# Expert weights in 16 KB buffers and runs, and the last expert's second weight by halves of its rows

## The chip, the cores and the metric

The kernel runs on one core of a Trainium2 chip. The metric is device time in microseconds (us) of one execution; the span runs from the first to the last instruction that the profile shows. TensorE, VectorE, ScalarE, GpSimd and SyncE are PE, DVE, ACT, POOL and SP in the rows. SP issues almost all transfers.

## The reference

One transformer-like block over 256 tokens of width 1024 (a gated linear recurrence and a spatial gating branch), then a mixture of experts with the top 4 of 32, then a norm. All numbers are fp32. The expert part, which is most of the work:

```python
def expert_block(args):
    xblk, e = args
    z = xblk @ w1[e] + b1[e]                       # 1024 x 2048
    gate = jnp.minimum(z[:, :D_EXPERT], SWIGLU_LIMIT)
    lin = jnp.clip(z[:, D_EXPERT:], -SWIGLU_LIMIT, SWIGLU_LIMIT)
    return (gate * jax.nn.sigmoid(SWIGLU_ALPHA * gate) * (lin + 1.0)) @ w2[e] + b2[e]   # 1024 x 1024
```

Each expert has 8 MiB of w1 and 4 MiB of w2, 384 MiB in all; every expert is computed for its selected tokens (up to 64 in the usual path).

## The kernel before

**The front stage** (up to about 500 us) computes modulation, recurrence, gating, branches, output projection and router. Its weights come in granules of 1 MiB, 1024 rows by 256 columns, that is in runs of 1 KB. A granule is split into a high and a low part by ScalarE and VectorE (L241, L242), which frees its buffer, and is used in 48 products (L321).

**The buffers.** `wtile` hands out 8 KB (per partition) buffers in a fixed rotation, the list `slots`. It begins with three (`ring`); after the third granule of section 6 seven more join it (`ringb`, `LATER` = 3), which lie where the attention's tiles were. At the expert stage four more (`d0` to `d3`) and one for a single use (`big1`) follow when the tiles in them are done, and five of `ringc`, where the front stage's pools were. So 20 MiB can be in before TensorE frees a buffer.

**The expert stage.** For each expert e TensorE opens two accumulators with the bias (L791), multiplies the gathered tokens with eight loads of w1 (`w1_step`, L800, one load is 128 rows by 2048 columns, an 8 KB run on each partition), with the scatter of an earlier expert (L852) and on odd experts the gather for the next two (L769) between them. VectorE and ScalarE make the gated product, meanwhile TensorE multiplies expert e-1 with its four loads of w2 (`w2_steps`, L836, again 8 KB runs), and then turns the gated product of e (L818). The order on TensorE is the order of the code (`manual_schedule`); on SP and the other engines the scheduler sets the order, and SP then issues strictly in it. A load waits on SP until the last reader of its buffer is done, and for the load eight issues before it.

**The last expert's w2** (`last_columns`) comes as four column blocks of 256, each in two half-MiB transfers with 1 KB runs; each block is multiplied (L868), scaled (L871), scattered (L876, L877), squared for the norm on ScalarE (L879) and multiplied by the norm's gain (L880). Then the norm and the output.

Of the kernel before, what the change touches and what calls it, by code (L numbers as in the profile page):

```python
# [8 lines left out]
F32 = mybir.dt.float32  # L9
# [22 lines left out]
def kernel(  # L32
# [174 lines left out]
    def mod_col(j, h, res):  # L207
        a, step = mod_sums(j, h)

        def finish():  # L210
            step(1)
            pt = bank("tp", (P, 4, 2))
            for k in range(4):
                te.matmul(pt[:, k], a[:, k * P:(k + 1) * P], ones[:, 0:2], start=True, stop=True)
            ve.tensor_add(res[:, 4 * h:4 * h + 4], pt[:, :, 0], bmcol[:, 8 * j + 4 * h:8 * j + 4 * h + 4])
        return [lambda: step(0), finish]
# [134 lines left out]

    pack2 = pack_rows("pack2", [(rows(norm2_g), 8), (rows(lb_fwd), 16), (rows(lb_bwd), 16), (rows(gnorm_g), 1), (b_s[0], 8)])
    cols2 = unpack(pack2, "cols2")
    n2col, gncol = cols2[:, 0:8], cols2[:, 40:41]
# [179 lines left out]
    for j in range(5):  # L534
# [22 lines left out]
        if j == 0:  # L557
# [11 lines left out]
            nc.sync.dma_start(wr_sb, w_router[0].rearrange("(k p) e -> p k e", p=P))  # L569
# [20 lines left out]
    def more_slots(n):  # L590
        if n == LATER:
            slots.extend([(ringb, "w")] * RING_B)

    more_slots(0)
# [4 lines left out]
    for j in range(4):  # L599
        pp = two(win(6, j), hT[0], True)  # L600
        more_slots(j + 1)
# [14 lines left out]
    for j in range(4):  # L616
        pp = two(win(5, j), hT[0], False)
        more_slots(j + 5)
# [54 lines left out]
    for j in range(4):  # L673
# [14 lines left out]
        for k in range(2):  # L688
            for tt in range(2):
                te.transpose(pt[:, k, tt * P:(tt + 1) * P], acc[:, tt, (2 * j + k) * P:(2 * j + k + 1) * P], ident)  # L690
# [56 lines left out]
    slots[4:4] = [(consts, f"d{i}") for i in range(4)] + [(consts, "big1")]  # L747
    slots += [(ringc, "w")] * RING_C
# [46 lines left out]
    def w1_step(zz, xT, kt, src):  # L795
        w = wtile([P, 2 * D])
        nc.sync.dma_start(w, src)
        for n in range(2):
            for h in range(2):
                te.matmul(zz[n][h * C:(h + 1) * C], xT[:, kt], w[:, n * D + h * 512:n * D + (h + 1) * 512],  # L800
# [22 lines left out]
    def w2_steps(hT2, selb, w2e):  # L823
# [33 lines left out]
    def last_columns(j, hT2, pT, selb, wcol, w2e):  # L857

        selb = selb.to_broadcast([96, C])
        s = slice(j * 256, (j + 1) * 256)  # L860
        w = wtile([P, KT, 256])
        for h in range(2):
            nc.sync.dma_start(w[:, 4 * h:4 * h + 4], w2e[:, h, :, s])
        py = bank2(("py", "misc")[j % 2], (P, 256))
        te.matmul(py[0:C], selb, b3[:, 2, s], start=True, stop=False, skip_group_check=True)
        for kt in range(KT):
            h = kt % 2
            te.matmul(py[h * C:(h + 1) * C], hT2[:, kt % 4, (kt // 4) * C:(kt // 4) * C + C], w[:, kt],  # L868
                      start=kt == 1, stop=kt >= KT - 2, skip_group_check=True)
        y = wk.tile([P, 256], F32, name="y")  # L870
        ve.tensor_mul(y, py, g2bc[:, s])  # L871

        def rest():
            for tt in range(2):
                pc = bank2((("sc0", "sc1"), ("gate", "lin"))[j % 2][tt], (P, 256))
                te.matmul(pc, pT[:, tt * P:(tt + 1) * P], y, start=True, stop=True)  # L876
                ve.scalar_tensor_tensor(acc[:, tt, s], pc, wcol[tt], acc[:, tt, s], op0=OP.mult, op1=OP.add)  # L877
# [171 lines left out]
```

## Time and profile before

| | |
|---|---|
| median of 3 runs | 1451.46 us (1450.17 to 1451.85) |
| profiled execution | 1452.21 us, span 1450.4 us |
| TensorE busy | 1345.7 us, 93% of the span |
| VectorE, ScalarE, GpSimd busy | 640.0, 307.9, 161.1 us |
| SP's transfers | 483.37 MB, 84.3% of the 16 transfer engines' span |
| mean granted TensorE clock | 0.984 |

A busy share is an average over stages with different limits: the front stage and the expert stage have to be read apart.

### The profile page before, as it was taken

To read this page: it belongs to the slowest core of one execution; us is meant where nothing else is said; L and a number is where in the kernel's file an instruction comes from. 1 tells how busy PE (TensorE), PEld (TensorE's weight loads), DVE (VectorE), ACT (ScalarE), POOL (GpSimd) and SP (SyncE) were. 2 spreads that over 40 slices of the span, in tenths; PEclk is the share of its full clock that TensorE was granted. 3 is DMA by queue.
4 is the path that set the end of the run, shared out by engine and by line. 5 is a ranking of instruction groups with operands and counts; after the bars stand their busy time and mean duration, and the time that the engine had idled before them with its cause. 6 is when DMAs were issued, how large, how long until landed. Compare 5 with 4: busy or idle time off the path is not lost. (4 is left out here: it accounts for less than half of the span.)

```text
span 1450.4 us, 19638 instructions
## 1 busy us (share of the span) xinstructions
PE 1345.7 (93%) x8218; PEld 743.0 (51%) x8218; DVE 640.0 (44%) x1108; ACT 307.9 (21%) x497; POOL 161.1 (11%) x109
## 2 busy tenths in 40 slices
PE   6979798979999999999999999999999999899996
PEld 4979787878999843333333332323323233232323
DVE  5498888887768613222222322222222222222223
ACT  2463354454444310100000000100001000010001
POOL 3054323240064000000000000000000000000001
PEclk8999999999999999999999999999999999999999
DMA  9536252534995899999999999999999999999994
GB/s 333 188 116 204 88 195 67 201 120 162 292 295 220 312 388 414 420 420 421 421 420 420 420 421 420 421 420 421 421 420 421 420 421 422 420 420 421 420 419 173
DMA packets 130751, 487.43 MB, mean 336 GB/s; under 512 B 9161, under 2 KB 71746, under 8 KB 82018
## 3 DMA queue, kind: packets, MB, share of 16 engines
q1 hardware_dynamic: 129810, 483.37, 84.3%
q0 software_dynamic: 848, 2.75, 0.6%
q8 instruction: 66, 1.08, 0.3%
q14 instruction: 27, 0.22, 0.0%
HBM read 485.04 MB, written 1.05 MB: 335 GB/s over the span
## 5 line engine op out<-in xcount | busy, mean ns | idle before, releaser
L800 PE MATMUL gate<-w,xT 128*64 128x512 f32 x1024 | 270.4, 606 | 18.6 <-DMA w<-in_w_dram 17.2
L800 PE MATMUL lin<-w,xT 128*64 128x512 f32 x1024 | 263.5, 592 | 0.0
L836 PE MATMUL py<-w,hT 128*64 128x512 f32 x992 | 228.1, 597 | 20.8 <-DMA w<-in_w_dram 20.8
L321 PE MATMUL acc<-hh,ghi 128*128 128x256 f32 x576 | 166.9, 290 | 12.1 <-ACT iv L394 12.1
L855 DVE SCALAR_TENSOR_TENSOR acc<-sc,wts,acc 128x512 f32<-128x512 f32 x124 | 87.4, 746 | 205.3 <-PE sc L852 205.3
L321 PE MATMUL acc<-hh,glo 128*128 128x256 f32 x576 | 165.5, 288 | 11.3 <-DVE glo L242 11.3
L321 PE MATMUL acc<-hl,ghi 128*128 128x256 f32 x576 | 165.1, 287 | 0.0
L242 DVE TENSOR_TENSOR glo<-w,ghi 128x1024 fp32r<-128x1024 f32 (+1 forms) x99 | 139.1, 1409 | 50.2 <-ACT ghi L241 49.8
L836 PEld LDWEIGHTS py<-w,hT 128*64 128x64 f32 x992 | 66.3, 136 | 162.8 <-issue 98.6
L800 PEld LDWEIGHTS lin<-w,xT 128*64 128x64 f32 x1024 | 74.3, 137 | 145.5 <-issue 145.5
L800 PEld LDWEIGHTS gate<-w,xT 128*64 128x64 f32 x1024 | 61.0, 136 | 163.6 <-issue 96.6
L241 ACT ACTIVATE ghi<-w 128x1024 fp32r<-128x1024 f32 (+1 forms) x102 | 102.4, 1007 | 144.3 <-PE acc L321 106.6
L321 PEld LDWEIGHTS acc<-hh,ghi 128*128 128x128 f32 x576 | 111.4, 194 | 13.3 <-ACT iv L394 12.5
L321 PEld LDWEIGHTS acc<-hh,glo 128*128 128x128 f32 x576 | 111.3, 193 | 13.0 <-DVE glo L242 12.8
L321 PEld LDWEIGHTS acc<-hl,ghi 128*128 128x128 f32 x576 | 111.4, 193 | 0.7 <-issue 0.7
L839 DVE TENSOR_TENSOR y<-py,g2h 128x512 f32<-128x512 f32 x31 | 21.4, 691 | 188.1 <-PE py L836 188.1
L925 POOL DMA_DIRECT2D bc<-in_final_g_dram x1 | 0.6, 557 | 934.3 <-DMA w<-in_w_dram 934.3
L773 ACT ACTIVATE xT<-misc,sh,a 128x128 f32<-128x128 f32 (+1 forms) x68 | 30.7, 451 | 272.4 <-DVE xT L775 272.4
L807 DVE TENSOR_SCALAR g<-gate 128x512 f32<-128x512 f32 x32 | 22.1, 691 | 147.1 <-PE gate L800 147.1
L321 PE MATMUL acc<-ghi,hh 128*128 128x256 f32 x256 | 73.3, 288 | 14.0 <-DVE og L383 6.4
L775 DVE TENSOR_SCALAR xT<-misc,a,sh 128x128 f32<-128x128 f32 (+1 forms) x68 | 27.2, 401 | 131.0 <-PE misc L769 120.5
L808 ACT ACTIVATE s<-g 128x512 f32<-128x512 f32 x32 | 20.2, 630 | 292.5 <-DVE g L807 292.5
(316 smaller groups left out, 1732.4 us busy)
## 6 DMA issues: line engine op xcount, KB each, us to landing
w<-in_w_dram SPq DMA_DIRECT2D x380, 1024.0 KB, 19.8
w<-in_w_in_dram SPq DMA_DIRECT2D x33, 1024.0 KB, 5.6
w<-in_w_mod_dram SPq DMA_DIRECT2D x24, 1024.0 KB, 6.6
w<-in_w_branch_a_dram SPq DMA_DIRECT2D x4, 1024.0 KB, 16.2
w<-in_w_branch_b_dram SPq DMA_DIRECT2D x4, 1024.0 KB, 12.2
w<-in_w_out_dram SPq DMA_DIRECT2D x4, 1024.0 KB
w<-in_w_dram SPq DMA_DIRECT2D x8, 512.0 KB, 8.7
w<-in_w_in_dram SPq DMA_DIRECT2D x12, 256.0 KB, 7.5
```

Of the source, the lines that this page charges most:

```text
L241: sc.activation(hi, src, AF.Copy)
L242: eng.tensor_sub(lo, src, hi)
L321: te.matmul(o, l, r, start=opens and kt == 0 and n == 0, stop=kt == KT - 1 and n == 2, skip_group_check=True)
L773: sc.activation(xT[:, kt], pg[:, k], AF.Identity, bias=sh2[:, kt:kt + 1], scale=a2[:, kt:kt + 1])
L775: ve.tensor_scalar(xT[:, kt], pg[:, k], a2[:, kt:kt + 1], sh2[:, kt:kt + 1], op0=OP.mult, op1=OP.add)
L800: te.matmul(zz[n][h * C:(h + 1) * C], xT[:, kt], w[:, n * D + h * 512:n * D + (h + 1) * 512], start=False, stop=kt == KT - 1, skip_group_c ...
L807: ve.tensor_scalar(g, zz[0], 7.0, None, op0=OP.min)
L808: sc.activation(s, g, AF.Sigmoid, scale=1.702)
L836: te.matmul(py[h * C:(h + 1) * C], hT2[:, kt % 4, (kt // 4) * C:(kt // 4) * C + C], w[:, k, h * 512:(h + 1) * 512], start=False, stop=kt = ...
L839: ve.tensor_mul(y, py, g2h)
L855: ve.scalar_tensor_tensor(acc[:, tt, s], pcs[h], wcol[tt], old[:, tt, s], op0=OP.mult, op1=OP.add)
L925: gp.dma_start(fgbc, bcast(final_g, D))
```

## The change

- At the expert stage the list becomes three double buffers of 16 KB (`ringb`), the three single ones, `d0` to `d3`, `big1`, and three double ones (`ringc`): again 20 MiB. `ringb` no longer serves granules: the front stage keeps three buffers to its end.
- `two_units` loads 2 MiB: as one transfer into a double buffer where the next entry of the list is one, and otherwise as two transfers into two single buffers. `wtile` takes the first entry of the wanted size.
- The rows of w1 are taken in pairs, row 256 j + 2 p + k on partition p, so that a double load has one run of 16 KB on each partition; w2 has it with four rows of 4 KB. A single load still has 8 KB runs. The order of the 1024 inner rows follows in x1's transposes and gathers (read in steps of two elements), in the modulation's columns (`cols3`) and in the router's weights (four transfers).
- The last expert's w2 comes as four blocks of 1 MiB: 512 columns by half of the rows, in 2 KB runs.

The core of the diff:

```diff
-    slots = [(ring, "w")] * RING_A
-
-    def wtile(shape):
-
-        pool, tag = slots.pop(0)
+    slots = [(ring, "w", 1)] * RING_A
+
+    def wtile(shape, units=1):
+
+        i = next(i for i, s in enumerate(slots) if s[2] == units)
+        pool, tag, _ = slots.pop(i)
         if tag != "big1":
-            slots.append((pool, tag))
+            slots.append((pool, tag, units))
         return pool.tile(shape, F32, name="w", tag=tag)
+
+    def two_units(src, n):
+
+        r = 4096 // n
+        if slots[0][2] == 2:
+            w = wtile([P, r, n], 2)
+            nc.sync.dma_start(w, src)
+            return w[:, :r // 2], w[:, r // 2:]
+        ws = [wtile([P, r // 2, n]) for _ in range(2)]
+        for i, w in enumerate(ws):
+            nc.sync.dma_start(w, src[:, i * (r // 2):(i + 1) * (r // 2)])
+        return ws
...
-    def more_slots(n):
-        if n == LATER:
-            slots.extend([(ringb, "w")] * RING_B)
...
-    slots[4:4] = [(consts, f"d{i}") for i in range(4)] + [(consts, "big1")]
-    slots += [(ringc, "w")] * RING_C
+    slots[:] = ([(ringb, "w", 2)] * RING_B + slots + [(consts, f"d{i}", 1) for i in range(4)] + [(consts, "big1", 1)] +
+                [(ringc, "w", 2)] * RING_C)
...
-                    te.matmul(pg[:, k], x1[:, tt, kt * P:(kt + 1) * P], tok[:, tt], start=tt == 0, stop=tt == 1)
+                    te.matmul(pg[:, k], view(x1, tt * D + kt // 2 * 256 + kt % 2, [[2, P]]), tok[:, tt], start=tt == 0, stop=tt == 1)
...
-            w = wtile([P, 2, D])
-            nc.sync.dma_start(w, w2e[:, k2 // 2, k2 % 2 * 2:k2 % 2 * 2 + 2])
+            if k2 % 2 == 0:
+                ws = two_units(w2e[:, k2 // 2], D)
+            w = ws[k2 % 2]
...
-    w1e = lambda e, kt: w1[0, e, kt * P:(kt + 1) * P]
+    w1e = lambda e, j: w1[0, e, j * 256:(j + 1) * 256].rearrange("(p k) n -> p k n", k=2)
...
             for kt in range(KT):
-                w1_step(zz, xTs[e], kt, w1e(e, kt))
+                if kt % 2 == 0:
+                    ws = two_units(w1e(e, kt // 2), 2 * D)
+                w1_step(zz, xTs[e], kt, ws[kt % 2])
...
-        rest = last_columns(0, hT2, pT, sel(e), wcols(e), w2e(e))
+        first, last = (last_columns(c, hT2, pT, sel(e), wcols(e), w2e(e)) for c in range(2))
+        first[0]()
         scatter(*ready[1:])
-        for j in range(1, 4):
-            then = last_columns(j, hT2, pT, sel(e), wcols(e), w2e(e))
-            rest()
-            rest = then
-        rest()
+        first[1]()
+        last[0]()
+        first[2]()
+        last[1]()
+        last[2]()
...
-RING_B = 7
-RING_C = 5
+RING_B = 3
+RING_C = 3
```

In the new `last_columns` the second half of a column block is multiplied and finished in one piece of 512 columns for the first block and in two of 256 for the last.

**The order on SP, end of the front stage.** Before, the last granules (w_out) are issued ahead of the first expert loads; `w` with a number is a load in the order of the code:

```order
L293 DMA w_5132<-in_w_out_dram 128x8x256 [waits DMAHW2_49,DVE_49]
L293 DMA w_5210<-in_w_out_dram 128x8x256 [waits DMAHW3_49,DVE_49]
L293 DMA w_5288<-in_w_out_dram 128x8x256 [waits DMAHW4_49,DVE_49]
L797 DMA w_5503<-in_w1_dram 128x2048 [waits DMAHW5_49,DVE_49]
L797 DMA w_5509<-in_w1_dram 128x2048 [waits DMAHW6_49,DVE_49]
```

Now three double loads of expert 0 stand between the third and the fourth granule of section 5 (w_4137 and w_4208), ahead of 16 further granules:

```order
L306 DMA w_4066<-in_w_in_dram 128x8x256 [waits DMAHW5_49,DMAHW0_49,DVE_49]
L306 DMA w_4137<-in_w_in_dram 128x8x256 [waits DMAHW6_49,DVE_49]
L58 DMA w_5515<-in_w1_dram 128x4096 [waits DVE_49,Pool_49]
L58 DMA w_5525<-in_w1_dram 128x4096 [waits DVE_49,PE_49]
L58 DMA w_5550<-in_w1_dram 128x4096
L306 DMA w_4208<-in_w_in_dram 128x8x256 [waits DMAHW7_49,DVE_49]
L306 DMA w_4279<-in_w_branch_b_dram 128x8x256 [waits DMAHW0_49,DVE_49]
```

Six MiB moved ahead of the fourth granule.

**The order on SP, expert stage.** Before, it is the order of the code; here the four loads of w2 of expert 28 and the first of w1 of expert 30:

```order
L832 DMA w_9336<-in_w2_dram 128x2048 [waits DMAHW5_49,PE_49]
L832 DMA w_9342<-in_w2_dram 128x2048 [waits DMAHW6_49,PE_49]
L832 DMA w_9348<-in_w2_dram 128x2048 [waits DMAHW7_49,PE_49]
L832 DMA w_9354<-in_w2_dram 128x2048 [waits DMAHW0_49,PE_49]
L797 DMA w_9375<-in_w1_dram 128x2048 [waits DMAHW1_49,PE_49]
```

Now the same place (w_9138, w_9139 and the double w_9150 are w2 of expert 28, w_9175 to w_9217 w1 of expert 30, w_9242 to w_9253 w2 of expert 29):

```order
L62 DMA w_9138<-in_w2_dram 128x2048 [waits DMAHW3_49,DMAHW2_49,PE_49]
L58 DMA w_9150<-in_w2_dram 128x4096 [waits PE_49]
L58 DMA w_9175<-in_w1_dram 128x4096 [waits DMAHW4_49,PE_49]
L58 DMA w_9191<-in_w1_dram 128x4096 [waits DMAHW5_49,PE_49]
L58 DMA w_9207<-in_w1_dram 128x4096 [waits DMAHW6_49,PE_49]
L58 DMA w_9217<-in_w1_dram 128x4096 [waits DMAHW7_49,PE_49]
L58 DMA w_9242<-in_w2_dram 128x4096 [waits DMAHW0_49,PE_49]
L62 DMA w_9139<-in_w2_dram 128x2048 [waits DMAHW1_49,PE_49]
L62 DMA w_9252<-in_w2_dram 128x2048 [waits DMAHW2_49,PE_49]
```

w_9139 moved behind six double loads that come after it in the code. The same stands once in each round of the list, 17 times from w_5844 (expert 3) to w_9139; at expert 31 a load, w_9323, stands behind three double loads.

**The order on TensorE, same place.** The products of expert 28's w2 keep the order of the code:

```order
L851 MATMUL py_9135<-w_9138,hT2_9025 64x512 [waits DMAHW2_49]
L851 MATMUL py_9135<-w_9138,hT2_9025 64x512 x3
L851 MATMUL py_9135<-w_9139,hT2_9025 64x512 [waits DMAHW1_49]
L851 MATMUL py_9135<-w_9139,hT2_9025 64x512 x3
L851 MATMUL py_9135<-w_9150,hT2_9025 64x512 [waits DMAHW3_49]
```

Nothing moved here: TensorE waits for w_9139 ahead of w_9150.

## Rows read from the trace of the kernel before

**Rows 1.** The page's head and slices of 36 us.
```profile
span 1450.4 us, 19638 instructions
...
GB/s 333 188 116 204 88 195 67 201 120 162 292 295 220 312 388 414 420 420 421 421 420 420 420 421 420 421 420 421 421 420 421 420 421 422 420 420 421 420 419 173
```

**Rows 2.** Stretches: length, busy PE, PEld, DVE, ACT, POOL, clock, transfer share, GB/s.
```profile
384.00:400.00 16.00, 16.00 (x139) 16.00 (x138) 12.81 (x16) 7.06 (x11) 0.00 (x0) 1.00 1.09 348
600.00:800.00 200.00, 200.00 (x968) 71.60 (x966) 56.76 (x100) 15.30 (x28) 0.00 (x0) 1.00 1.01 421
...
1000.00:1100.00 100.00, 91.48 (x419) 29.77 (x417) 24.16 (x41) 6.11 (x11) 0.00 (x0) 1.00 1.01 421
```

**Rows 3.** TensorE in order of time, experts 5 and 6, and L940.
```profile
634.03 0.41 PE L791 MATMUL gate<-b,sel 96*64 96x512 bf16 x2
...
655.45 7.03 PE L836 MATMUL py<-w,hT 128*64 128x512 f32 x32
662.41 0.75 PE L818 MATMUL misc<-ident,l 128*128 128x128 f32 x4
663.09 0.41 PE L791 MATMUL gate<-b,sel 96*64 96x512 bf16 x2
...
687.89 0.41 PE L791 MATMUL gate<-b,sel 96*64 96x512 bf16 x2
...
1403.24 1.13 PE L940 MATMUL misc<-g2h,ident 128*128 128x512 f32 x2
```

**Rows 4.** TensorE in order of time, later.
```profile
851.38 0.75 PE L818 MATMUL misc<-ident,l 128*128 128x128 f32 x4
...
1420.88 1.94 PE L836 MATMUL py<-w,hT 128*64 128x512 f32 x8 [0.62 <-DMA w<-in_w_dram]
1422.74 0.75 PE L818 MATMUL misc<-ident,l 128*128 128x128 f32 x4
```

**Rows 5.** The page's issues: count, size of one, median us to landing.
```profile
w<-in_w_dram SPq DMA_DIRECT2D x380, 1024.0 KB, 19.8
```

**Rows 6.** The page's packets, counted up to each size.
```profile
DMA packets 130751, 487.43 MB, mean 336 GB/s; under 512 B 9161, under 2 KB 71746, under 8 KB 82018
```

**Rows 7.** SP's issues in order of time.
```profile
371.75 12.00 SPq L293 DMA_DIRECT2D w<-in_w_branch_b_dram  x4
...
436.07 60.45 SPq L797 DMA_DIRECT2D w<-in_w_dram  x16
500.77 2.08 SPq L832 DMA_DIRECT2D w<-in_w_dram  x4
```

**Rows 8.** TensorE in order of time, expert 1's last w1 product.
```profile
546.31 1.03 PE L800 MATMUL lin<-w,xT 128*64 128x512 f32 x4
```

**Rows 9.** The w1 loads of L797 by source.
```profile
DMA to landing us min/median/max: 4.8/19.8/21.4
```

**Rows 10.** ScalarE's splits in order of time.
```profile
371.72 1.06 ACT L241 ACTIVATE ghi<-w 128x1024 fp32r<-128x1024 f32 x1 [1.26 <-PE acc L321]
...
385.85 1.06 ACT L241 ACTIVATE ghi<-w 128x1024 fp32r<-128x1024 f32 x1 [1.78 <-PE acc L321]
...
393.37 1.06 ACT L241 ACTIVATE ghi<-w 128x1024 fp32r<-128x1024 f32 x1 [2.21 <-issue]
```

**Rows 11.** Stretches around a gap of TensorE in the front stage.
```profile
100.00:104.00 4.00, 3.33 (x17) 3.37 (x18) 4.00 (x5) 0.62 (x2) 2.74 (x2) 0.54 0.00 0
104.00:108.00 4.00, 4.00 (x36) 4.00 (x35) 4.00 (x7) 2.63 (x6) 0.00 (x0) 1.00 0.00 0
```

**Rows 12.** TensorE in order of time, first and last products at the lower clock.
```profile
100.67 0.55 PE L321 MATMUL acc<-ghi,hh 128*128 128x256 f32 x1 [6.37 <-DVE og L383]
...
103.57 0.32 PE L321 MATMUL acc<-ghi,hl 128*128 128x256 f32 x1
```

**Rows 13.** First product of the last blocks, and VectorE's start of the norm.
```profile
1424.18 1.95 PE L868 MATMUL py<-w,hT 128*64 128x256 f32 x16 [0.25 <-ACT hT L820]
...
1441.68 0.16 DVE L1000 TENSOR_REDUCE fss<-ss 128x2 f32<-128x8 f32 x1 [0.64 <-ACTq L960]
```

More of the change, by code (lines that the diff above doesn't have):

```diff
@@ L350 @@
             dense(g, four_outs(pps, natural), natural, ((2 * q, 2),), ve if q else gp)
+    pack3 = late.tile([12, 256], F32, name="pack3")
+    for i, src in enumerate((norm2_g[0], b_mod[0, 3 * D:4 * D], b_mod[0, 4 * D:5 * D])):
+        nc.sync.dma_start(pack3[4 * i:4 * i + 4], src.rearrange("(r f) -> r f", f=256))
+    cols3 = consts.tile([P, 3, KT], F32, name="cols3")
+    pt = bank("tp", (P, 2, 12))
+    for k in range(2):
+        te.transpose(pt[:, k], view(pack3, k, [[2, P]]), ident[:12, :12])
+    ve.tensor_copy(cols3.rearrange("p i (j k) -> p i j k", k=2), pt.rearrange("p k (i j) -> p i j k", i=3))
+    n2col = cols3[:, 0]
     pack2 = pack_rows("pack2", [(rows(norm2_g), 8), (rows(lb_fwd), 16), (rows(lb_bwd), 16), (rows(gnorm_g), 1), (b_s[0], 8)])
     cols2 = unpack(pack2, "cols2")
-    n2col, gncol = cols2[:, 0:8], cols2[:, 40:41]
+    gncol = cols2[:, 40:41]
     lb, omlb = [], []
@@ L855, in scatter, with last_columns @@
                 ve.scalar_tensor_tensor(acc[:, tt, s], pcs[h], wcol[tt], old[:, tt, s], op0=OP.mult, op1=OP.add)
-    def last_columns(j, hT2, pT, selb, wcol, w2e):
+    def last_columns(c, hT2, pT, selb, wcol, w2e):
         selb = selb.to_broadcast([96, C])
[L860 to L871, printed above, removed]
-        def rest():
[L874 to L877, printed above, removed]
-                junk = wk.tile([P, 256], F32, name="junk", tag="g", bufs=1)
-                sc.activation(junk, acc[:, tt, s], AF.Square, accum_out=ss8[:, tt, j:j + 1])
-                (gp if j < 3 else ve).tensor_mul(accg[:, tt, s], acc[:, tt, s], fgbc[:, s])
-        return rest
@@ new lines, in last_columns, with products @@
+        py = bank2(("py", "misc")[c])
+        y = wk.tile([P, 512], F32, name="y")
+        blocks = [slice(0, 512)] if c == 0 else [slice(0, 256), slice(256, 512)]
+        def products(u):
+            if u == 0:
+                te.matmul(py[0:C], selb, b3[:, 2, c * 512:(c + 1) * 512], start=True, stop=False, skip_group_check=True)
+            w = wtile([P, 4, 512])
+            nc.sync.dma_start(w, w2e[:, u, :, c * 512:(c + 1) * 512])
+            for b in blocks if u else [slice(0, 512)]:
+                for k in range(4):
+                    h = k % 2
+                    te.matmul(py[h * C:(h + 1) * C, b], hT2[:, k, u * C:u * C + C], w[:, k, b],
+                              start=u == 0 and k == 1, stop=u == 1 and k >= 2, skip_group_check=True)
+                if u:
+                    ve.tensor_mul(y[:, b], py[:, b], g2bc[:, c * 512 + b.start:c * 512 + b.stop])
@@ new lines, in rest @@
+        def rest():
+            for i, b in enumerate(blocks):
+                n = b.stop - b.start
+                s = slice(c * 512 + b.start, c * 512 + b.stop)
+                for tt in range(2):
+                    pc = bank2((("sc0", "sc1"), ("gate", "lin"))[(c + i) % 2][tt], (P, n))
+                    te.matmul(pc, pT[:, tt * P:(tt + 1) * P], y[:, b], start=True, stop=True)
+                    ve.scalar_tensor_tensor(acc[:, tt, s], pc, wcol[tt], acc[:, tt, s], op0=OP.mult, op1=OP.add)
+                    junk = wk.tile([P, n], F32, name="junk", tag="g", bufs=1)
+                    sc.activation(junk, acc[:, tt, s], AF.Square, accum_out=ss8[:, tt, c + i:c + i + 1])
+                    (ve if i else gp).tensor_mul(accg[:, tt, s], acc[:, tt, s], fgbc[:, s])
@@ L883 @@
+        return [lambda: products(0), lambda: products(1), rest]
     tok, xTs = {}, {}
@@ L922 @@
                 slots[:] = [x for x in slots if x[1] not in ("d0", "d1")]
+                assert slots[0][2] == 2 or sum(x[2] == 1 for x in slots) >= 2
                 bc = consts.tile([P, 2, D], F32, name="bc", tag="d0")
@@ L992 @@
         for tt in range(2):
-            for j in range(4):
-                s = slice(j * 256, (j + 1) * 256)
-                junk = wk.tile([P, 256], F32, name="junk", tag="g", bufs=1)
+            for j, s in enumerate((slice(0, 512), slice(512, 768), slice(768, 1024))):
+                junk = wk.tile([P, s.stop - s.start], F32, name="junk", tag="g", bufs=1)
                 sc.activation(junk, acc[:, tt, s], AF.Square, accum_out=ss8[:, tt, j:j + 1])
@@ L1014 @@
 FIRST = 6
-LATER = 3
 MOD_POOL = (0,)
```

24 lines of the change are left out of this document (11 added, 13 removed).

## The prediction

> **What bounds the kernel now.** I first read the page's slices. From about 500 us to 1430 us the transfers run at 419 to 422 GB/s [rows 1]: the expert stage streams its weights at one rate to the end. The windows then show that this is not TensorE's bound at first: from 600 to 800 us TensorE is busy all the time at the same 421 GB/s, from 1000 to 1100 us only 91.48 of 100 us [rows 2]. So the first experts eat a stock of loads that are already there, and after it is used up each product waits for its load. The timeline of TensorE shows both. Without waits two experts take 687.89 - 634.03 = 53.86 us, 2.24 us for each of 24 loads of 1 MiB; the one with gathers takes 29.06 us, the one without 24.80 us [rows 3]. Later the group of L836 at 1420.88 stands behind a wait of 0.62 us for its load, and from the turn (L818) of expert 12 at 851.38 to that of expert 31 at 1422.74 there are 571.36 us for 19 experts, 2.506 us a load [rows 4]. After 1420.88 no load is late: the rest (29.5 us of the span) is a chain of TensorE, VectorE and ScalarE.
>
> Two further facts matter. Loads land in the order of issue: the median from issue to landing is 19.8 us, eight times 2.49 us [rows 5], and each load waits for the eighth before it. And an 8 KB run is one packet: 130751 - 82018 = 48733 packets are of 8 KB or more [rows 6], and 380 loads of 128 rows are 48640.
>
> **The rate: what a 16 KB run saves.** The trace has no run of 16 KB. It has 1 KB runs at 348 GB/s (384 to 400 us) and 8 KB runs at 421 GB/s, both with the transfer engines full [rows 2]. One engine of 16 thus takes 1024/21.75 = 47.1 ns and 8192/26.3 = 311.3 ns for a packet: 0.03686 ns a byte and 9.35 ns a packet. With 16 KB runs a MiB has 4 packets fewer on each engine, 0.0374 us saved of 2.506. Bounds: nothing (a run is cut in two packets), and 0.075 us (the packet's cost vanishes). I take 0.0374, what the two rows give. The Trainium skill (DMA: Bandwidth & Descriptors, section Why small descriptors are slow) puts the fixed overhead at some 3 cycles a packet. At that page's 850 MHz these are 3.5 ns, an estimate by which a MiB would save 0.014 us and the sum below would end at 1467.8 in place of 1463.1; the rows do not agree with it (9.35 ns), and I go by them.
>
> **The order: what the buffers do to it.** 114 double loads carry 228 of the 380 MiB; 152 stay single. The seven single buffers come round on their own, so the eighth single load in a round reuses the buffer of the first. The order on SP shows what becomes of that: the load is put behind the next six double loads, 12 MiB after its place, while TensorE still asks for it in its old place. So TensorE waits at this load until it lands, finds the next 12 MiB there, works through them without a wait (2.24 us each against some 2.48 of the stream), and waits again at the next such load. A round is 20 MiB: the stream needs 20 x 2.506 - 12 x 0.037 = 49.7 us, TensorE 44.9, so it idles some 4.8 us a round, at one place instead of at most loads. While rounds follow each other this costs nothing. It costs at the end: at the last late load that TensorE waits for (w_9139, the second MiB of expert 28's second weight, the 366th MiB in the order of issue, 14 from the end) it is some 13 MiB behind the stream, and no waits are left to lose.
>
> When does w_9139 land? I anchor the stream where it is held by TensorE. Six MiB go ahead of the front stage's last granules, at 371.75 us, when the attention's memory is free; in the kernel before the first expert load goes out at 436.07 and 20 are out at 502.85 [rows 7]. So the stock is full earlier, but it is the same 20 MiB, and then the stream follows the releases. By about 546 us 33 MiB are in (the 20, the last of them issued at about 501 us as before, and 13 whose buffers expert 0 and the first half of expert 1 free); the next double load needs the buffer read by expert 1's last two w1 products, released at 546.31 + 1.03 = 547.3 [rows 8]. The kernel before has, counted back from 1420.9 at 2.506 us, 32 MiB in at that time: a lead of about 1 MiB is all that the early start leaves. From issue to a first landing the least is 4.8 us [rows 9], 2.3 more than the transfer.
>
> The six MiB also delay granules in the front. The fourth granule of section 5 follows them: its buffer is free after a split that starts at 371.72 (about 374.4 with VectorE's part), but its transfer begins when 6 x 2.46 us after 373.0 are over, so it lands at 391.6. Its split, at 385.85 in the kernel before, ends at 394.1; its products begin when the copy at 393.37 can [rows 10]. So I count 0.7 us of delay. Bounds: 0, and 5 us if the following granules are late too; those are issued up to three granules ahead and need 3.0 us of transfer each (1 MiB at 348 GB/s), so I take 0.7.
>
> The sum: 547.3 + 0.7 + 2.3 + 333 MiB x 2.506 (834.5) - 204 MiB x 0.0374 (7.6) = 1377.2 us for w_9139. Behind it TensorE has three MiB of L836 (6.97/4 = 1.74 each, from 655.45 to 662.41: 5.2), the turn (0.68), expert 30 without gathers (24.80) and expert 31, the same with two products of L940 (2 x 1.05) [rows 3]: 57.6 us, to 1434.8. No load is late in it: the 14 MiB behind it and the four last blocks are there by about 1425. The same point of the kernel before is 1422.74 + 0.68 = 1423.4: **11.4 us later**.
>
> The clock: after 6.37 us idle, the products from 100.67 us on come at a granted 0.54 (1.2 GHz), and 1.00 (2.4 GHz) is back 2.9 us later [rows 11, 12]: about 1.4 us lost. A wait of 4 to 5 us may do it; in all rounds but the last the next wait absorbs it. Between 0 and 1.4 I take 0.7.
>
> **The tail.** From 1424.18 to 1441.68 the kernel before has TensorE and VectorE in turn, and its eight half-MiB loads are not waited for [rows 13]. The four new blocks have the same products in groups of 512 columns, two openings with the bias fewer, and the last two 256-column pieces end in the same chain of VectorE and ScalarE. I take -0.5 us; bounds -2 and +1.5.
>
> **Costed at nothing:** x1 read in steps of two elements (gathers and router: hidden in the 4.8 us of a round, and none is in the last 57.6 us), pack3 and the four router loads (front; TensorE is busy there and waits for none of them), the gates' place in it.
>
> Sum: 11.4 + 0.7 - 0.5 = +11.6 on a span of 1450.4, 1462.0. The profiled execution took 1452.21, 1.81 more than its span and 0.75 over the median of the runs: as a median, **1463.1 us**.
>
> **The rivals.**
> - *The late loads hold nobody* (faster). If they landed ahead of the double loads, the stream alone would decide: its last MiB at 550.3 + 347 x 2.506 - 210 x 0.0374 = 1412.0, 8.9 us ahead of 1420.9, and with the tail 1442. For it: TensorE is busy without a break up to 800 us [rows 2]. Against it: the landing times [rows 5] and the wait written on w_9139's product. It decides if w_9139 is there 11.6 us earlier, by 1365.6.
> - *The run of 16 KB saves little*, cut in two or limited elsewhere: 7.6 us back, 1470.7. For it: two run lengths always lie on one line, so nothing in the trace proves the line up to 16 KB. Against it: nothing in the trace splits a run of 8 KB. (By the Trainium skill's 3 cycles, named above, it would be the 1467.8.)
> - *The packet's cost vanishes*: 1455.4.
> - *The front is held* by the six MiB for 5 us in place of 0.7: 1467.4.
>
> **How the numbers follow.** The forecast (1458 to 1468) has 0.52, little saving 0.20, late loads harmless 0.12, packet cost gone 0.08, front held 0.06, something else 0.02. The range reaches from the vanishing packet cost less 2 us of tail, 1453, to no saving and the tail's upper bound, 1472, and leaves out the harmless order. Slower by over 0.2% (2.9 us, about what can be told from no change) is above 1454.4: 0.82; within it 0.06; faster 0.12.
>
> **What would show it.** Right: TensorE's waits for weights are some 16 to 18 of 3 to 7 us, at single loads, from about 630 us on; windows near 426 GB/s where double loads pass; no wait on a load after about 1377 us, and the transfers idle from about 1425. Wrong: many waits of 0.5 us up to 1410 us (loads not late), an unchanged 421 GB/s, or a first expert product several us later than in the kernel before.

## The result, and the profile after

The changed kernel takes 1473.45 us (median of 4 runs, 1467.77 to 1474.9), the kernel before beside it 1450.82 (1450.06 to 1451.85): a ratio of 1.0148, with a 95% interval of 1.012 to 1.0176. The direction is that of the forecast, the size is twice it (+22.6 us in place of +11.6). The ratios, here and below, are not the quotients of the medians (here that would be 1.0156); the two differ by up to 0.15%. The profiled execution took 1474.9 us, the slowest of the four; its span is 1473.1 against the 1450.4 of before.

The page of the changed kernel: head, slices of 37 us, packets, and the expert loads with their size and the median time to landing.

```profile
span 1473.1 us, 19304 instructions
...
GB/s 333 183 112 203 88 197 89 170 133 154 333 213 233 328 403 381 426 423 422 426 426 423 422 426 426 420 424 427 423 423 423 426 408 422 426 426 423 423 332 33
DMA packets 111781, 487.42 MB, mean 331 GB/s; under 512 B 6821, under 2 KB 65322, under 8 KB 77642
...
w<-in_w_dram SPq DMA_DIRECT2D x114, 2048.0 KB, 15.9
w<-in_w_dram SPq DMA_DIRECT2D x156, 1024.0 KB, 16.1
```

A 16 KB run is one packet: 111781 - 77642 = 34139 are of 8 KB or more, and 114 double and 152 single loads of 128 runs are 34048 (before: 48733 [rows 6]). Slices of 426 and 422 alternate where [rows 1] had 420 and 421. So the streaming did become faster, and the kernel is slower all the same.

Stretches of the changed kernel, with the same columns as [rows 2]:

```profile
380.00:400.00 20.00, 18.27 (x154) 17.88 (x154) 13.85 (x29) 8.54 (x11) 2.20 (x4) 1.00 0.95 351
400.00:420.00 20.00, 18.63 (x157) 18.43 (x156) 17.02 (x13) 7.47 (x8) 15.45 (x12) 1.00 0.78 257
600.00:800.00 200.00, 191.61 (x905) 69.88 (x903) 52.55 (x98) 15.91 (x30) 0.00 (x0) 0.97 1.01 424
1000.00:1100.00 100.00, 94.44 (x455) 34.94 (x453) 26.01 (x49) 7.94 (x15) 0.00 (x0) 0.98 1.01 424
1384.00:1388.00 4.00, 2.15 (x8) 0.73 (x10) 0.07 (x1) 0.00 (x0) 0.00 (x0) 0.89 1.01 420
1388.00:1392.00 4.00, 4.00 (x16) 1.27 (x14) 0.00 (x0) 0.00 (x0) 0.00 (x0) 0.68 1.02 424
```

The first two in the kernel before:

```profile
380.00:400.00 20.00, 20.00 (x173) 20.00 (x172) 16.16 (x27) 9.60 (x13) 0.00 (x0) 1.00 1.09 348
400.00:420.00 20.00, 20.00 (x168) 19.83 (x168) 14.51 (x12) 8.21 (x9) 13.25 (x10) 1.00 1.05 335
```

Three things are new. TensorE, which in the kernel before is busy for all 40 us from 380 to 420, has 3.1 us of holes there. From 600 to 800 us, where it had no wait at all [rows 2], it is idle for 8.4 us. And the granted clock, 1.00 before, is 0.97 there; from 1388 to 1392 us, behind a wait, its mean is 0.68, so a part of this stretch is at 1.2 GHz and the rest at 2.4.

TensorE in order of time, at the places that set the end:

```profile
396.33 1.16 PE L640 MATMUL o_ps<-wsT,v 128*128 128x128 f32 x8 [0.78 <-DVE t L643]
...
398.67 0.39 PE L334 MATMUL acc<-hh,glo 128*128 128x256 f32 x1 [0.95 <-DVE glo L255]
...
413.18 0.39 PE L334 MATMUL acc<-hl,ghi 128*128 128x256 f32 x1 [1.37 <-DVE hl L255]
...
513.20 1.08 PE L814 MATMUL gate<-w,xT 128*64 128x512 f32 x4
...
520.21 2.10 PE L785 MATMUL misc<-p,acc 128*128 128x64 f32 x16
...
533.63 1.11 PE L832 MATMUL misc<-ident,l 128*128 128x128 f32 x4 [2.12 <-DVE l L825]
...
535.52 1.87 PE L814 MATMUL gate<-w,xT 128*64 128x512 f32 x4
...
555.11 7.03 PE L851 MATMUL py<-w,hT 128*64 128x512 f32 x32
...
590.95 1.08 PE L814 MATMUL gate<-w,xT 128*64 128x512 f32 x4 [1.06 <-DMA w<-in_w_dram]
...
640.83 8.14 PE L851 MATMUL py<-w,hT 128*64 128x512 f32 x24 [3.69 <-DMA w<-in_w_dram]
...
1336.12 1.97 PE L814 MATMUL gate<-w,xT 128*64 128x512 f32 x4 [4.55 <-DMA w<-in_w_dram]
...
1385.85 7.07 PE L851 MATMUL py<-w,hT 128*64 128x512 f32 x24 [1.97 <-DMA w<-in_w_dram]
1392.85 0.75 PE L832 MATMUL misc<-ident,l 128*128 128x128 f32 x4
...
1444.86 0.75 PE L832 MATMUL misc<-ident,l 128*128 128x128 f32 x4
```

The kernel before, at the same gather between the first w1 products and at the turn of expert 0 with the product behind it:

```profile
514.82 2.00 PE L769 MATMUL misc<-p,acc 128*128 128x64 f32 x16
...
528.04 0.75 PE L818 MATMUL misc<-ident,l 128*128 128x128 f32 x4 [2.12 <-DVE l L811]
...
529.17 1.03 PE L800 MATMUL gate<-w,xT 128*64 128x512 f32 x4
```

The late loads are there as forecast: TensorE waits for a load at 590.95 us, at 640.83 and from there every 49.67 us on average up to w_9139 at 1385.85 (15 rounds in 745.02 us; one of them, near 690 us, shows no wait), and no load is waited for behind it. The waits are 0.4 to 6.1 us long, where 3 to 7 were forecast. But everything is later than forecast: the first w1 product comes at 513.20 (507.81 before), w_9139 lands 8.7 us behind the 1377.2 of the sum, and the 24 products behind it take 7.07 us in place of 5.2.

### One table for all runs

The executions of this kernel differ by some us in the early front stage, whatever is changed in the expert stage: the same program text there had its first w1 product at 507.81 in the kernel before and at 513.83 in the run tail_only below. The difference lies early: counted from the last products of the attention (L506, at 359.11 and 364.98 us) it comes after 148.70 us in the one and 148.85 in the other. So the runs are compared by stretches between fixed instructions: point A is the start of the first w1 product, B that of expert 0's first w2 product, C that of the last turn (expert 31). Each row is one profiled execution, read from the order in time of TensorE as above (changed kernel: 513.20, 555.11, 1444.86).

| kernel | A | A to B | B to C | C to end | median us |
|---|---|---|---|---|---|
| before | 507.81 | 39.91 | 875.02 | 27.66 | 1450.82 |
| changed | 513.20 | 41.91 | 889.75 | 28.24 | 1473.45 |
| even_singles | 515.49 | 42.00 | 871.73 | 27.98 | 1457.86 |
| runs_8k | 512.51 | 41.94 | 896.28 | 27.57 | 1481.97 |
| loads_behind | 507.18 | 41.91 | 888.05 | 27.96 | 1467.25 |
| tail_only | 513.83 | 39.92 | 874.68 | 28.27 | 1452.66 |
| even_behind | 507.26 | 40.30 | 870.77 | 27.47 | 1452.78 |
| interleaved | 507.75 | 40.31 | 875.06 | 27.58 | 1455.42 |
| all_double | 505.34 | 40.31 | 872.41 | 27.94 | 1451.28 |
| filled_waits | 511.98 | 41.54 | 891.15 | 28.03 | 1473.02 |
| all_double_early | 518.49 | 41.56 | 874.21 | 27.64 | 1455.20 |
| filled_short | 513.32 | 40.37 | 888.38 | 28.03 | 1473.16 |
| before_less | 503.96 | 41.55 | 877.67 | 27.82 | 1453.85 |
| even_halves | 515.21 | 41.92 | 870.47 | 27.80 | 1450.10 |

The change costs 5.4 us ahead of A, 2.0 from A to B, 14.7 from B to C and 0.6 behind C: 22.7 us. The forecast had 0.7, 0, 11.4 (0.7 of it for the clock) and -0.5.

### The profile page after: what moved, and what is told of

Read it like the earlier page. It is cut to its first block, busy times and chain, and to the rows that moved or that the text cites. A ratio compares the mean times of both kernels' runs of the same rounds, so it can differ in the third digit from the quotient of the medians.

```text
span 1473.1 us, 19304 instructions
## 1 busy us (share of the span) xinstructions
PE 1355.8 (92%) x8190; PEld 756.0 (51%) x8190; DVE 642.2 (44%) x1106; ACT 307.8 (21%) x493; POOL 160.3 (11%) x107
## 2 busy tenths in 40 slices
DMA packets 111781, 487.42 MB, mean 331 GB/s; under 512 B 6821, under 2 KB 65322, under 8 KB 77642
## 5 line engine op out<-in xcount | busy, mean ns | idle before, releaser
L814 PE MATMUL gate<-w,xT 128*64 128x512 f32 x1024 | 275.3, 617 | 39.6 <-DMA w<-in_w_dram 39.6
L814 PE MATMUL lin<-w,xT 128*64 128x512 f32 x1024 | 269.8, 606 | 0.0
L851 PE MATMUL py<-w,hT 128*64 128x512 f32 x992 | 223.9, 603 | 10.5 <-DMA w<-in_w_dram 10.5
L334 PE MATMUL acc<-hh,ghi 128*128 128x256 f32 x576 | 167.9, 292 | 10.3 <-ACT iv L416 10.3
L255 DVE TENSOR_TENSOR glo<-w,ghi 128x1024 fp32r<-128x1024 f32 (+1 forms) x99 | 137.0, 1388 | 56.7 <-ACT ghi L254 56.3
L814 PEld LDWEIGHTS gate<-w,xT 128*64 128x64 f32 x1024 | 65.1, 139 | 176.2 <-issue 116.4
L851 PEld LDWEIGHTS py<-w,hT 128*64 128x64 f32 x992 | 70.1, 139 | 143.5 <-issue 122.4
L334 PEld LDWEIGHTS acc<-hh,ghi 128*128 128x128 f32 x576 | 111.8, 194 | 11.6 <-ACT iv L416 10.7
L785 PEld LDWEIGHTS misc<-p,acc 128*128 128x128 f32 x544 | 67.5, 199 | 28.2 <-issue 27.5
```

The lines of the kernel that those rows point to most:

```text
L255: eng.tensor_sub(lo, src, hi)
L334: te.matmul(o, l, r, start=opens and kt == 0 and n == 0, stop=kt == KT - 1 and n == 2, skip_group_check=True)
L785: te.matmul(pg[:, k], view(x1, tt * D + kt // 2 * 256 + kt % 2, [[2, P]]), tok[:, tt], start=tt == 0, stop=tt == 1)
L814: te.matmul(zz[n][h * C:(h + 1) * C], xT[:, kt], w[:, 0, n * D + h * 512:n * D + (h + 1) * 512], start=False, stop=kt == KT - 1, skip_grou ...
```

## The experiments

### even_singles: no late loads

```diff
-        if tag != "big1":
+        if tag not in ("big1", "d3"):
             slots.append((pool, tag, units))
```

> The changed kernel, with the buffer d3 used for one load only, like big1. The six single buffers left then come round in pairs of the same round, no single load reuses a buffer that was filled seven loads ago, and the loads on SP stand in the order of the code. Stock in the later rounds: 18 MiB in place of 19. Theory A (the late single loads at the end of the stage are what costs): TensorE waits a little at most loads, and the stream's end decides. In the changed kernel w_9139, the 366th MiB, lands at 1385.85; 14 MiB more at 2.47 us end at 1420.4, the last products and the turn at about 1423 instead of 1445.5, so the median falls by some 22 us to about 1451 (1447 to 1455). Rival B (late loads hold nobody, the time went into the front and the clock): within 3 us of 1473. Rival C (half of it): the single that is gone makes the stream wait for TensorE: 1458 to 1468, with windows of the transfers below 415 GB/s.

Measured: 1457.86 us (12 runs; 1.0035 of the kernel before, 1.0015 to 1.0055). TensorE in order of time, the end:

```profile
1425.64 3.65 PE L851 MATMUL py<-w,hT 128*64 128x512 f32 x16 [1.31 <-DMA w<-in_w_dram]
1429.22 0.75 PE L832 MATMUL misc<-ident,l 128*128 128x128 f32 x4
```

TensorE again waits a little at many loads up to the last, and B to C falls by 18.0 us, from 889.75 to 871.73; the median falls by 15.6. So the late loads are what costs, as theory A has it: rival B is out, and the sign of rival C, transfers below 415 GB/s, is not there (425 from 600 to 800 us). The median misses the theory's 1447 to 1455 all the same: of the 22 us expected, 4 are missing from B to C, 2.65 of them for the MiB of stock given up (before_less, below). Point A is no earlier than in the changed kernel (this profile has it 2.3 later): the front is a cost of its own.

### runs_8k: the price of a packet

```diff
-            nc.sync.dma_start(w, src)
+            for i in range(2):
+                nc.sync.dma_start(w[:, i * (r // 2):(i + 1) * (r // 2)], src[:, i * (r // 2):(i + 1) * (r // 2)])
```

> The changed kernel, same buffers and same places on SP, but each double buffer is filled by two transfers of 1 MiB whose runs are 8 KB. Theory (a 16 KB run saves one packet's cost, 0.0374 us a MiB): 204 MiB of double loads ahead of w_9139 cost 7.6 us more, windows fall from 426 to 421 GB/s where double loads pass, median about 1481 (1478 to 1484). Rival (16 KB runs save little): 1473 plus or minus 2, windows unchanged. Rival (the packet's cost vanishes, 0.075 us a MiB): 1488. The number of loads that may be under way is eight in both, here eight MiB in place of up to sixteen; if that matters the slower side shows it too, as holes between loads in the windows.

Measured: 1481.97 us (6 runs; 1.0213, 1.0178 to 1.0248), within the theory's 1478 to 1484. Stretches:

```profile
600.00:800.00 200.00, 187.73 (x900) 69.17 (x900) 52.55 (x98) 15.91 (x30) 0.00 (x0) 0.98 1.01 420
1000.00:1100.00 100.00, 93.19 (x445) 34.56 (x443) 25.09 (x47) 7.94 (x15) 0.00 (x0) 0.97 1.01 419
```

420 and 419 GB/s where the changed kernel has 424. The waits at both ends of the fifteen rounds:

```profile
640.98 5.37 PE L852 MATMUL py<-w,hT 128*64 128x512 f32 x24 [3.67 <-DMA w<-in_w_dram]
...
1393.42 5.37 PE L852 MATMUL py<-w,hT 128*64 128x512 f32 x24 [1.10 <-DMA w<-in_w_dram]
```

The fifteen rounds between the same waits take 752.44 us (640.98 to 1393.42) in place of 745.02, with 180 MiB of double loads in them: 7.42/180 = 0.041 us a MiB, where the line through the runs of 1 KB and 8 KB had given 0.0374. The term of the sum was right in size. What it is the price of is not separated: the edit doubles the packets and the transfers alike. In favour of the packets: the line through the runs of 1 KB and 8 KB, both in transfers of 1 MiB, gives nine tenths of it. The 0.014 us that the Trainium skill's 3 cycles a packet give (DMA: Bandwidth & Descriptors, section Why small descriptors are slow; an estimate at that page's 850 MHz) would have been 2.5 us over these rounds; the measured 7.42 decides against it.

### loads_behind: the front

```diff
         ve.tensor_mul(m, pp, t)
+        if j < 3:
+            w = ringb.tile([P, 2, 2 * D], F32, name="w", tag="w")
+            ve.tensor_copy(w[:, 0, 0:1], m[:, 0, 0:1])
+            nc.sync.dma_start(w, w1[0, 0, j * 256:(j + 1) * 256].rearrange("(p k) n -> p k n", k=2))
```

The three are handed out first, and the list of buffers then begins with the single ones and ends with these three.

> The changed kernel, with the first three double loads tied behind the first three products with branch_a in the front stage (one element of each buffer is written from their result first), so that six MiB no longer stand ahead of the fourth granule of section 5. Theory (the six MiB hold the front): TensorE has no gaps between 390 and 415 us, the first product with w1 comes at 508 to 509 us in place of 513.2, the late loads stay, and the median falls by the same 4 to 5 us to about 1469. Rival (three buffers for granules alone hold the front, not the loads): first product at 511 us or later, median within 2 us of 1473. Rival (the loads come too late for expert 0): the first product is early but TensorE waits at loads ahead of 560 us, and the gain is lost.

Measured: 1467.25 us (5 runs; 1.0096, 1.0063 to 1.0128). Stretches:

```profile
380.00:400.00 20.00, 20.00 (x173) 20.00 (x172) 15.62 (x23) 9.73 (x14) 0.00 (x0) 1.00 0.51 162
400.00:420.00 20.00, 20.00 (x169) 20.00 (x168) 15.31 (x14) 7.07 (x8) 15.00 (x13) 1.00 0.77 238
```

The 40 us have no hole, with the same three buffers for granules, and A is at 507.18. Counted from the last products of the attention (L506, L528 and L532, at 359.11, 359.51 and 357.77 us), A comes after 148.7 us in the kernel before, 153.7 in the changed one and 149.4 here. The other kernels agree: 153.6 to 154.3 us in the four with the six MiB in their early place, 148.6 to 149.8 in the seven without. So it is the six MiB, with 4.3 of the 5.0 us, and not the three buffers by themselves. The median falls by 6.2 us. In the changed kernel SP's issues come in this order:

```profile
370.36 2.29 SPq L58 DMA_DIRECT2D w<-in_w_dram  x3
374.58 0.38 SPq L306 DMA_DIRECT2D w<-in_w_in_dram  x1
380.22 24.23 SPq L306 DMA_DIRECT2D w<-in_w_branch_b_dram  x4
```

and ScalarE's splits follow:

```profile
383.57 1.06 ACT L254 ACTIVATE ghi<-w 128x1024 fp32r<-128x1024 f32 x1 [1.30 <-PE acc L334]
...
394.02 0.60 ACT L636 ACTIVATE t<-acc 128x512 f32<-128x512 f32 x1 [2.73 <-DVE t L643]
...
395.29 1.99 ACT L254 ACTIVATE ghi<-w 128x1024 fp32r<-128x1024 f32 x2
```

The granule behind the six MiB goes out at 374.58. Its split begins at 395.29, where the kernel before has it at 385.85 [rows 10] and the sum had it end at 394.1; VectorE's part ends at 398.61, and the product that waits for it starts at 398.67. The next four splits come 4.4 to 6.7 us later than in the kernel before, and the products stall three times up to 413.18 (3.1 us; the rest of the 5.0 does not show as holes). In the kernel before, with ten buffers, the granules behind it had been on their way (335 GB/s from 400 to 420 us, 257 here). This link between the six MiB and the stalls is read from the rows and not tested by itself; the order of work has a part in it, since ScalarE takes the split only behind an operation for which it waits until 394.02.

### tail_only: the last blocks

The new last_columns, with its order of calls, in the kernel before (the two last parts of the diff, nothing else).

> The kernel before, with nothing of the change but the last expert's second weight in four 1 MB blocks of 512 columns by half of the rows. From the end of the last turn to the end of the span the kernel before takes 27.0 us. The prediction's step: -0.5 us (bounds -2 and +1.5), median about 1450.3. The changed kernel's own trace says 27.6 us: +0.6, 1451.4. Rival (the larger pieces put more of the chain behind the last product): +1.5 us or more, 1452.5. All three are within what a measurement can tell; the profile's stretch from the turn to the end decides.

Measured: 1452.66 us (0.9999, 0.998 to 1.0017), and C to end 28.27 us against 27.66, as the changed kernel's 28.24. The gain of 0.5 us is not there. Whether the new blocks cost something cannot be told: the table has 27.5 to 28.3 us behind C for the kernels with them, and 27.7 and 27.8 for the two without.

### even_behind: both repairs

The diffs of even_singles and loads_behind together.

> Both repairs together: the first three double loads tied behind products with branch_a, and d3 used for one load only, so that the singles come in pairs and no load is late. Measured apart: 1473.45 with neither, 1467.25 with the first, 1457.9 with the second. Theory (two separate causes, which add): 1457.9 - 6.2 = 1451.7, or up to 2 us less, because the run with the second alone had its first w1 product at 515.5 us, 2.3 later than the changed kernel: 1449 to 1452, no different from the kernel before. Rival (the early loads and the late ones are one cause, a fuller stock): 1456 or more. If the 16 KB runs bring what the windows say (0.041 us a MiB on two thirds of the loads, some 9 us), the turn of expert 31 would come ahead of the 1423.4 of before by what is not lost to two MiB less stock (4 to 5 us) and to the last load being 2 MiB long (1.7 us).

Measured: 1452.78 us (1.0019, 1.0003 to 1.0035). The causes add: A as in loads_behind, B to C near that of even_singles (870.77 and 871.73). Against the kernel before, B to C is 4.25 us shorter. By the page it has 127 double loads; some 230 MiB of them fall in this stretch (an estimate: two rounds less than all), worth some 9.5 us at 0.041. So over 5 us were given back; the last two runs ask where.

### interleaved: late by less

```diff
+            if e == 2:
+                s1, s2 = [x for x in slots if x[2] == 1], [x for x in slots if x[2] == 2]
+                slots[:] = (s2[0:1] + s1[0:2] + s2[1:2] + s1[2:4] + s2[2:3] + s1[4:6] + s2[3:4] + s1[6:7] + s2[4:6])
```

on top of loads_behind.

> The three double loads tied behind branch_a as in the run before, all 19 MiB of buffers kept, and from expert 2 on the list of buffers interleaved (double, two singles, double, two singles, ...). On SP one single load a round then stands behind three double loads (6 MiB) in place of six (12 MiB), some others behind one. Theory (what a late load costs is what TensorE is behind the stream at the last of them): about half of the 15.6 to 22 us that taking all late loads away brings, on 1467.25: 1454 to 1460. Rival (any late load costs alike): 1467 plus or minus 2. Rival (late by three doubles is hidden by the stock): 1448 to 1452.

Measured: 1455.42 us (1.0032, 1.0015 to 1.005), within the theory's 1454 to 1460. B to C is 875.06: 13 us less than with loads six doubles late (888.05), 4.3 more than with none (870.77). The last of the late loads:

```profile
1367.73 3.44 PE L860 MATMUL py<-w,hT 128*64 128x512 f32 x8 [3.87 <-DMA w<-in_w_dram]
```

even_behind has a MiB of stock less. With the 2.65 us that before_less gives for it, lateness by three doubles costs some 7 us and by six some 20 (an estimate), and 1.5 of the 7 are the clock, since the 8 products take 3.44 us in place of 1.94. So the dose matters: half the lateness costs about a third, by this one run.

### all_double and all_double_early: nine double buffers

Nothing but double buffers, the front's single ones in a pool that is given up (early: that pool and the others in another order).

```diff
-    ring = ctx.enter_context(tc.tile_pool(name="ring", bufs=RING_A))
+    ring = p1.enter_context(tc.tile_pool(name="ring", bufs=RING_A))
+    dd = p1.enter_context(tc.tile_pool(name="dd", bufs=1))
...
+    slots[:] = [(ringc, "w", 2)] * RING_C + [(ringc, "x", 2)] + [(ringb, "w", 2)] * RING_B
```

> The loads tied behind branch_a, and all weight buffers of the expert stage double (nine, 18 MiB: the singles of the front stage lie in a pool that is given up for them); the last two loads of expert 30's second weight are issued in halves of 1 MiB, the four last blocks go into halves of two double buffers. No load is late. Theory: every MiB gains the 0.041 us that the runs of 8 KB against 16 KB showed: 347 MiB x 0.041 = 14.2 us ahead of the kernel before, 5 us lost to two MiB less of stock, the turn of expert 31 at about 1413 to 1415, median 1441 to 1444. Rival (the stream no longer bounds: TensorE waits 2 to 3 us at each double load): 1448 or more. Rival (the nine buffers come free too late at the start, 500 us in place of 470): first w1 product on time, but waits ahead of 600 us, 1450 or more.

> The kernel with nine double buffers, with its pools in another order, so that the six doubles of ringc lie first on the memory of the front stage's tiles and granules that are done earliest. In the run before, the transfers stood idle from 480 to 500 us (0 and 191 GB/s) with only four double loads issued, and then ran without a hole from 502 us to the end, so the stock was never full. Theory (the missing stock of some 5 to 6 MiB is what kept 0.041 us a MiB from showing): the transfers run at 390 GB/s or more from 480 to 500 us, holes appear between 530 and 560 us (the stock is full), the turn of expert 31 comes 6 to 12 us earlier than 1418.7, median 1439 to 1446. Rival (the rate gain ends at TensorE, which needs 27 us for the last expert whatever is there): the waits get shorter, the turn at 1416 or later, median 1449 or more. Rival (the new place makes the first expert's small tiles wait): first w1 product later than 508 us.

Measured: 1451.28 us (1.0007, 0.9991 to 1.0022) and 1455.20 (1.003, 1.0009 to 1.0052). The first, in stretches:

```profile
480.00:490.00 10.00, 10.00 (x88) 10.00 (x86) 5.24 (x8) 4.07 (x12) 0.00 (x0) 1.00 0.00 0
490.00:500.00 10.00, 9.81 (x70) 7.51 (x69) 6.15 (x30) 3.26 (x7) 0.00 (x0) 1.00 0.53 191
...
530.00:560.00 30.00, 30.00 (x155) 12.02 (x151) 7.50 (x16) 3.06 (x6) 0.00 (x0) 1.00 1.01 426
600.00:800.00 200.00, 196.93 (x947) 70.71 (x945) 55.48 (x99) 14.67 (x27) 0.00 (x0) 1.00 1.01 426
```

The rate is 426 GB/s (0.041 us a MiB off the 421 of before would make 428), but the transfers stand idle just ahead of the expert stage, because the buffers come free too late (SP waits there 15.6 us for VectorE's part of a split and 9.1 for products of the front), and run without a hole afterwards: the stock is never full, and TensorE is idle for 3.1 us between 600 and 800 us, where it was not in the kernel before. B to C is 2.6 us better than before, where 9 were expected (14 less 5 for two MiB of stock). The other pool order did not cure it; the idle stretch moved, and SP waits in it 26.6 us for the router's products:

```profile
490.00:500.00 10.00, 10.00 (x86) 10.00 (x86) 7.05 (x10) 5.42 (x13) 0.00 (x0) 1.00 0.23 95
500.00:510.00 10.00, 10.00 (x81) 9.27 (x81) 4.72 (x16) 3.60 (x11) 0.00 (x0) 1.00 0.01 2
```

Both expectations missed; the rival of all_double, buffers that come free too late, is what the stretches show. That a full stock would bring the gain stays open.

### filled_waits and filled_short: the clock

```diff
+    def fill(n):
+        t = bank2("misc")
+        for _ in range(n):
+            te.matmul(t, ident, g2h, start=True, stop=True)
...
+            if e == 0:
+                fill(4)
...
+            if late and k2 == 1:
+                fill(4)
```

(fill(2) in filled_short; late is expert 28.)

> The changed kernel with four more fp32 products of 128x512 (2.1 us, their result is not used) on TensorE in two of its waits: behind the last w1 product of expert 0 (2.12 us idle there, after which the changed kernel's products take 1.87 us in place of 1.03) and ahead of w_9139's product (1.97 us idle, after which 24 products take 7.07 us in place of 5.2). Theory (TensorE's clock falls to 1.2 GHz in these waits, and this costs 1.9 us at each place that no later wait absorbs): both groups run at 2.4 GHz, the end is 2 to 4 us earlier, about 1470. Rival (it is not the wait that lowers the clock): the same slow products, and 1473 to 1475.

> As the run with filled waits, with two fp32 products in place of four. There, four took 3.70 us in place of the 2.1 meant, so that they reached 1.5 us past the wait; the products behind them did run at the full clock (24 in 5.37 us in place of 7.07). Two take 1.85 us and end ahead of the load. Theory: full clock behind both waits and nothing pushed back: 1.7 to 2.0 us at each place, 1473.4 less 3 to 4 is 1469.5 to 1470.5. Rival (the 0.1 to 0.3 us left idle, or the front, decide): 1473 plus or minus 1.

Measured: 1473.02 and 1473.16 us. TensorE of filled_short in order of time:

```profile
1381.55 1.98 PE L841 MATMUL misc<-g2h,ident 128*128 128x512 f32 x4
1384.76 5.37 PE L859 MATMUL py<-w,hT 128*64 128x512 f32 x24 [1.23 <-DMA w<-in_w_dram]
1390.07 0.74 PE L832 MATMUL misc<-ident,l 128*128 128x128 f32 x4
```

The 24 products take 5.37 us in place of 7.07, with 1.23 us of idleness left ahead of them, and A to B is 40.37 in place of 41.91. So in the profile the price of the low clock is 1.5 us from A to B and 1.4 from B to C. loads_behind shows the second without any filling: the clock stays up behind its last late load, and B to C is 1.7 us shorter than in the changed kernel.

```profile
1379.83 5.37 PE L860 MATMUL py<-w,hT 128*64 128x512 f32 x24 [1.74 <-DMA w<-in_w_dram]
```

That the filling is what kept the clock up is less firm: it stayed up at all four filled places, but at expert 0's turn also in five of the eleven kernels that wait 2.12 us there without it. The medians do not show the gain; the runs of these kernels spread over 7 us and more (filled_short 1467.03 to 1476.62), so the time itself is inconclusive. In filled_waits the four products took 3.70 us and reached as far past the wait as the clock gave back.

### before_less and even_halves: what was given back

```diff
-        if tag != "big1":
+        if tag not in ("big1", "d3"):
```

in the kernel before, and in even_behind:

```diff
+            for i in range(2) if halves else ():
+                nc.sync.dma_start(w[:, i * (r // 2):(i + 1) * (r // 2)], src[:, i * (r // 2):(i + 1) * (r // 2)])
...
+                y = w2_steps(phT, sel(pe), w2e(pe), pe == E - 2)
```

> The kernel before, with the buffer d3 used for one load only: 18 MiB of stock in the later rounds in place of 19, all else as it was. It prices the MiB that the run with even singles gave up. From the first w1 product to the last turn the kernel before takes 914.93 us (507.81 to 1422.74). Theory (a MiB of stock less is one load less ahead when the stream starts to follow the releases, and this stays to the end): 2.2 to 2.5 us more, 917.3, median 1453.8. Rival (the stock is never short by one MiB): 915 plus or minus 0.5, median 1451.5.

> The kernel with both repairs (loads behind branch_a, singles in pairs), with the two last double loads, the second weight of expert 30, issued as two transfers of 1 MiB each into the halves of their buffers. In the run with both repairs the last load's 16 products (3.65 us) stand behind its landing; in the kernel before 8 (1.94). From the first w1 product to the last turn it took 911.07 us (507.26 to 1418.33). Theory (half of the last load is waited for less): 1.7 us less, 909.4, median 1451. Rival (the stream is not the last thing any more, or four runs of 8 KB cost what they did before): 910.5 to 911.5.

Measured: 1453.85 us (1.002, 0.9999 to 1.0041) and 1450.10 (0.9976, 0.9958 to 0.9994). A MiB of stock costs 2.65 us from B to C (877.67 against 875.02), near the 2.2 to 2.5 expected; the 1.6 us more from A to B are the clock, which fell in this execution. The halves bring 0.3 us from B to C and not 1.7: that expectation fell. Of the 5 us of even_behind, 2.65 are the stock; the rest stays open. even_halves is the only run with an interval below 1, and its median is 1.55 us below that of the kernel before beside it (1451.65), at the edge of what can be told. Its profile has 4.55 us less from B to C, 2.0 more from A to B (0.4 for the gathers, 1.6 for the clock) and 0.7 more from the attention to A.

## Why the prediction was wrong in size

- **The late loads** (the main term): right in place, spacing (49.67 us, forecast 49.7) and effect. Without them B to C is 18.0 us shorter, 20.7 with the 2.65 us of the MiB given up; the sum and its rival without late loads lay 20.3 apart (11.4 later against 8.9 earlier).
- **The rate**: right in size, 0.041 us a MiB for 0.0374; the rival of little saving and that of a vanishing packet cost are out.
- **The front**: this is the step that failed, "So I count 0.7 us of delay. Bounds: 0, and 5 us if the following granules are late too". They were late too: 5.0 us from 359 us to A (0.4 more lay ahead of it), and loads_behind shows the six MiB as the cause of 4.3. The split behind them began at 395.29, where the sum had it done by 394.1. I had taken the free transfer time behind the six MiB as enough, and not counted that the kernel before had its next granules in buffers already at that time. The rival that I gave 0.06 was the case: with it the forecast had been 1467.4.
- **The clock**: mis-sized and counted at one place of two. Behind w_9139 it cost 1.7 us (7.07 against the 5.37 of loads_behind and filled_short) where 0.7 stood, with 1.4 as the upper bound; behind expert 0's turn (533.63, 535.52) 1.6 us where nothing stood. There no later wait absorbs most of it: B to C is 888.05 us in loads_behind, where the clock fell at the turn, and 888.38 in filled_short, where it did not.
- **x1 in steps of two elements**, costed at nothing: 0.4 us from A to B, where TensorE waits for no load (40.3 in the kernels with this layout whose clock held, 39.9 without it). Each of the four gathers there takes 0.1 us more (2.10 against 2.00).
- **The tail**: +0.6 for -0.5 in the profiles of the changed kernel and tail_only, but kernels with the same tail differ by 0.8 among themselves: the gain is not there, and more cannot be told.
- What is left of B to C, some 2.3 of 889.75 us, is not explained. Some 1.8 of it is there at the first late load: by the terms of the sum and the delay measured at B it would land at 589.1 us (an estimate), and its product starts at 590.95. So the stream started later than the sum has it, at the rate forecast.

The sum with the measured terms: 5.4 + 2.0 + 14.7 + 0.6 = 22.7 on the span, against 11.6.

## What to carry to other kernels

A rotation of buffers of two sizes has to be followed for each size on its own: where an odd number of single buffers is taken in pairs, a load reuses a buffer that has just been filled, and the cost shows at the end of the stage and not where it arises. A larger transfer that is moved ahead of small ones delays not one of them but all whose head start it eats: compare how far ahead of their use they land, not only the sum of the transfer times. And a stream's gain of 1.6% (0.041 of 2.506 us) is soon given back to a smaller stock (2.65 us for one MiB).

## What the chip showed that I had not expected

- The same 2.12 us of idleness on TensorE at expert 0's turn is followed by products at 2.4 GHz in the kernel before, tail_only, even_behind, interleaved and all_double, and at 1.2 GHz in the changed kernel (granted 0.73 from 532 to 536 us), even_singles, runs_8k, loads_behind, before_less and even_halves, where the first four take 1.9 us in place of 1.03. In all_double_early 3.38 us of idleness there left the clock at 2.4 GHz (1.03 us). In the changed kernel waits of 1.77 and 2.04 us for a load (at 938.54 and 1087.94 us) left it at 2.4 GHz (24 products in 5.37 us), and 1.97 us at 1385.85 did not (7.07). So the length of a wait alone did not decide.
- From 8 KB to 16 KB a run saves about 10.3 ns a packet on one of 16 engines (0.0412 us a MiB, four packets fewer on each), if all of it is put down to the packets; between 1 KB and 8 KB it is 9.35 ns.
